# Four column tiles of one projection as a single group of seven products, and a merge by accumulating transfers

## The chip, the cores and the metric

One NeuronCore of a Trainium2 chip runs the kernel. Its engines work side by side, each through a queue of its own in a fixed order: TensorE (PE, with its weight loads shown as PEld), VectorE (DVE), ScalarE (ACT), GpSimd (POOL) and SyncE (SP), which here only issues transfers. Engines wait for one another by semaphores. The metric is the device time of the whole program in microseconds.

## The reference, cut to what matters

One layer of a hybrid encoder for 512 tokens and 2048 channels. Two branches, a sparse attention (A) and a retention (B), each give 1024 channels per token; both are projected to 2048 channels, gated, added, and go through one output projection:

```python
proj = h @ w_in
...
a_out = dsa_mixer(aq, ak, av, iq, ik, iw, positions, rel_bias) * jax.nn.silu(az)
...
b_out = retention_mixer(rq, rk, rv, ret_gn_gain) * jax.nn.silu(rz)
merged = jax.nn.sigmoid(ga) * (a_out @ w_a_out) + jax.nn.sigmoid(gb) * (b_out @ w_b_out)
r = x + merged @ w_o
return r + (p_i @ w_ple) * jax.nn.sigmoid(r @ w_ple_gate)
```

The change touches `sigmoid(ga) * (a_out @ w_a_out)`, its sum with branch B's share, and the start of `merged @ w_o`.

## The kernel before, in words

Activations lie transposed in SBUF: 128 channels on the partitions, 512 tokens along a row. Each float32 matrix is split into two float16 parts, high (`wh`, `ah`) and low (`wl`), and a product is three matmuls: high by high, high by low, low by high. ACT makes a high part (line 257 for weights, 475 and 481 for merged tiles), DVE the low part (`low_part`, line 143).

A column tile is 128 output channels; branch A's projection has 16, in the order 0, 8, 1, 9, 2, 10, ... 15 (`PAIRED`). A plain tile is `gemm`: 8 chunks of 128 input channels, three matmuls of 512 columns each (lines 337 to 339). Tiles 1 and 9, and 3 and 11, are pairs (`narrow`): `gemm_pair` with `nk=4` (line 443) splits input channels, output tiles and tokens into halves and forms the 2 by 2 block product by seven products of blocks instead of eight. Its weight blocks are sums and differences, made on the way by accumulating transfers from POOL (`add_block`, line 221) and by one DVE sum (line 268). The token side (`Xa`) is made by `a_sums` when the attention heads end. The seven products go to four PSUM banks `p`, `v`, `q`, `r`; ACT copies a bank at certain points (line 372) before PE adds to it again, and DVE combines banks and copies to the outputs (lines 378, 382, 1771). Every product is run in passes of one weight part; `RUNS` gives their order: the first two products high, the same low, the next two high, those and the fifth low, fifth and sixth high, sixth and seventh low, seventh high.

After a plain tile DVE multiplies by the gate from `sga` (line 1786) and adds branch B's share from `mbs` (line 1787); both were loaded by SP into one `B` buffer, of which there are five. When tiles k and k+8 are done, `x_step(k, 0..3)` makes the seven combinations of their token halves that the output projection needs (`sums`, lines 539 to 542, then high and low parts). The output projection is again `gemm_pair`, `nk=8`; its first group is `late`: its first four passes run over chunks 0 to 6, and then over chunk 7, which comes from tiles 7 and 15.

The order on every engine is that in which the code issues. A to-do list spreads the work: PE code calls `step()` after each chunk of a plain tile (8 a tile), after each pass of a `gemm_pair` with `nk=4` (14), and four times a pass with `nk=8` (56); each call runs what `later` made due and takes one item from the list `todo`, in which `None` is an empty place. Here `split_to(n)` makes weight parts up to unit n, and `load_to` issues their loads from SP, in order, into seven `wraw` buffers.

Of the kernel before, what the change touches and what calls it, by code (L numbers as in the profile page):

```python
# [19 lines left out]
L = 512  # L20
# [51 lines left out]

def block_kernel(tc, flag, cfg, xT, pT, posb, posq, w_in, w_v, w_r0, w_r1, w_ik, w_a, w_b, w_o, w_ple, w_gate,
                 w_gt, w_pt, fgb, tab, gains, cst, dec, out, out_a, out_b):
# [6 lines left out]
    with contextlib.ExitStack() as ctx:  # L81
# [278 lines left out]

        def gemm_pair(ids, X, done, late=False, turned=False, nk=8, more=None, compact=False):

# [6 lines left out]
            def copy(n, src):  # L369
                E[n] = U(n)  # L370
                cs = LO if compact else ALL
                act.activation(E[n][:, cs], src[:, cs], AF.Copy)  # L372

            def out(f, x, y, i, c):
                if compact:
                    return done(x[:, LO], y[:, LO], i, c, f)
                t = U("e_t")
                f(t, x, y)
                done(t[:, LO], t[:, HI], i, c)
# [12 lines left out]
            def first():  # L392
                if turned:
                    E["e1"] = U("e1")
                    act.activation(E["e1"][:, LO], p[:, LO], AF.Copy)
                else:
                    copy("e1", p)

            def second():
                if turned:  # L400
                    done(q[:, LO], E["e1"][:, LO], 0, LO)
                else:
                    out(f_q, q, E["e1"], 0, LO)
# [16 lines left out]
            for at, (n, part, ks) in enumerate(runs):  # L420
# [12 lines left out]
                for k in ks:  # L433
                    ended[n] += 1
                    x = X[PRODUCTS[n]][k]
                    if turned and isinstance(x, tuple):
                        moving = [(LO, v) for v in x[:2 - part]]
                    elif compact:
                        moving = [(LO, x[:, v]) for v in (LO, HI)[:2 - part]]
                    else:  # L440
                        moving = [(c, x[:, c])]
# [9 lines left out]
        def combos(lo, hi, name, keep=None, by=1.0, checked=False):  # L451
# [18 lines left out]
            def first_part(k):  # L470
                if k % 2 == 0:
                    one_of[0] = V2(name + "a11")
                t = X["a11"][k] = one_of[0][:, L * (k % 2):L * (k % 2) + L]
                s = lo(k)[:, LO]
                act.activation(t[:, LO], s, AF.Copy, scale=-by)
                lows.append(lambda: low_part(t[:, HI], s, t[:, LO], -by, checked))
# [167 lines left out]
        PAIRED = [m + 8 * i for m in range(8) for i in range(2)]  # L644
        u_wa.update((m, block(w_a[m], (8,))) for m in PAIRED if m % 8 not in narrow and m not in u_wa)
        u_d = [block_pair(w_o[m], w_o[m + 8]) for m in range(8)]
# [1111 lines left out]
        Xm, x_step = combos(lambda k: merged[k], lambda k: merged[k + 8], "m", by=cfg.m * un_a, checked=True)  # L1758
        for m in PAIRED:
            if m in narrow:  # L1760
                gate = []
                for n in (m, m + 8):
                    t = B("sm")
                    gate.append(t[:, 0:512])
                    merged[n] = t[:, 512:1024]
                    sp.dma_start(gate[-1], sga[n])
                    sp.dma_start(merged[n], mbs[n])
                have, pw = [0, 0], [U("wa"), U("wa")]

                def done(c0, c1, i, q, m=m, have=have, pw=pw, gate=gate):  # L1770
                    dve.tensor_add(pw[i][:, q], c0, c1)
                    have[i] += 1
                    if have[i] == 2:
                        o = merged[m + 8 * i]
                        dve.tensor_mul(pw[i], pw[i], gate[i])
                        dve.tensor_add(o, o, pw[i])

                gemm_pair(u_wn[m], Xa, done, turned=True, nk=4, more=lambda at: None)
            elif m - 8 not in narrow:
                t = B("sm")  # L1780
                s, o = t[:, 0:512], t[:, 512:1024]
                sp.dma_start(s, sga[m])
                sp.dma_start(o, mbs[m])
                merged[m] = o
                pw = gemm(u_wa[m], aparts, "ps_w")
                dve.tensor_mul(s, pw, s)
                dve.tensor_add(o, o, s)
            if m >= 8:
                k = m - 8
                gap = X_AFTER if k + 1 in narrow else X_BEHIND if k in narrow else (0, 0)  # L1790
                todo.extend([None] * gap[0])
                for i in (0, 1, 2, 3) if fast else (1, 0, 2, 3):
                    todo.extend([lambda k=k, i=i: x_step(k, i)] + [None] * gap[1])

# [409 lines left out]
OUTS_AT = (7, 7, 9, 9)  # L2204
X_AFTER, X_BEHIND = (5, 1), (2, 1)
LOOK = 3
# [20 lines left out]
def _layout(x, p, positions, w_in, norm_gain, w_a_out, w_b_out, w_o, ret_gn_gain,  # L2227
# [12 lines left out]
    o = {}  # L2240
# [14 lines left out]
    o["w_a"] = np.ascontiguousarray(tiles(np.asarray(w_a_out)[0])[:, :, A_ORDER])  # L2255
    o["w_b"] = tiles(np.asarray(w_b_out)[0])
    o["w_o"] = tiles(np.asarray(w_o)[0])
    o["w_ple"] = np.ascontiguousarray(
# [66 lines left out]
```

## Time and profile before

| | |
|---|---|
| median of 3 runs | 1543.59 us (1543.3 to 1544.23) |
| the profiled execution: time, span | 1543.44 us, 1541.6 us |
| granted TensorE clock, mean | 0.998 |
| PE busy | 1529.4 us, 99% |
| DVE busy | 1317.6 us, 85% |
| ACT busy | 970.0 us, 63% |
| POOL busy | 225.0 us, 15% |

The span runs from the first to the last instruction of the program; the time of the execution is 1.84 us longer. Matmuls are pipelined and their ends are modelled, so the pace of PE is read from starts. A row of the timeline merges like instructions that follow one another; in brackets stands the idle time of the engine ahead of it and what ended that.

### The profile page before, as it was taken

What the parts mean: (1) busy time and instruction counts of PE and PEld (TensorE: products, weight loads), DVE (VectorE), ACT (ScalarE), POOL (GpSimd) and SP (SyncE); (2) the same over time, 40 slices, a digit from 0 to 9 for tenths busy, and PEclk for the clock granted to TensorE, in tenths of its full rate; (3) what the DMA queues carried; (4) which work ended last, traced back from release to release, by engine and by line L of the source; (5) the groups of instructions that cost most, each with busy time, mean ns of one, the idle gap of its engine ahead of it and who ended that gap; (6) DMA issues with size and microseconds to landing.
All of it is one profiled execution on the core that took longest, in us unless ns stands there. A gap on an engine that the chain in (4) does not pass through costs nothing.

```text
span 1541.6 us, 27918 instructions
## 1 busy us (share of the span) xinstructions
PE 1529.4 (99%) x10433; PEld 986.7 (64%) x10433; DVE 1317.6 (85%) x2712; ACT 970.0 (63%) x1491; POOL 225.0 (15%) x261
## 2 busy tenths in 40 slices
PE   9999999999999999999999999999999999999997
PEld 5654446778878878876555666655555566547765
DVE  8899889888888888987788888788889999998975
ACT  7565545665666665687877766667633555576654
POOL 3000111111111111113431121200000111101101
PEclk9999999999999999999999999999999999999999
DMA  8436989899899899899999898999556899878974
GB/s 325 134 117 196 263 213 253 227 228 236 219 227 237 216 228 235 217 228 268 272 248 243 229 249 239 276 352 343 198 198 191 209 232 241 221 232 238 259 213 147
DMA packets 136274, 358.26 MB, mean 232 GB/s; under 512 B 22208, under 2 KB 34752, under 8 KB 136128
## 3 DMA queue, kind: packets, MB, share of 16 engines
q1 hardware_dynamic: 94368, 230.08, 43.1%
q0 software_dynamic: 28656, 101.20, 35.4%
q10 hardware_dynamic: 13104, 25.09, 4.4%
q8 instruction: 83, 1.36, 0.3%
q14 instruction: 63, 0.52, 0.1%
HBM read 311.76 MB, written 42.99 MB: 230 GB/s over the span
## 4 chain that ended last, share of the span: by engine, by line
PE 88%; DVE 6%; ACT 2%; issue 1%; DMA 1%; SPq 0%; DVEq 0%; ACTq 0%
PE ps_p L443 27%; PE ps_v L443 18%; PE ps_q L443 9%; PE ps_r L443 9%; PE ps_vn L1151 2%; PE ps_vn L1150 2%; PE ps_vn L1152 2%; PE ps_iq L339 1%; PE ps_iq L337 1%; PE ps_iq L338 1%; DVE wl L143 1%; ACT bm L1610 1%; PE ps_pg L2018 1%; PE ps_pg L2019 1%; PE ps_pg L2020 1%
## 5 line engine op out<-in xcount | busy, mean ns | idle before, releaser
L143 DVE SCALAR_TENSOR_TENSOR wl<-wraw,wh 128x1024 f16<-128x1024 f32 (+3 forms) x461 | 559.1, 1221 | 124.4 <-ACT wh L257 113.5
L257 ACT ACTIVATE wh<-wraw 128x1024 f16<-128x1024 f32 (+3 forms) x484 | 490.1, 1024 | 136.1 <-DVE wraw L268 74.8
L443 PEld LDWEIGHTS <-wh 128*128 128x128 f16 x4120 | 402.2, 98 | 239.0 <-issue 1.5
L443 PEld LDWEIGHTS <-wl 128*128 128x128 f16 x2968 | 289.4, 98 | 55.0 <-issue 0.2
L221 POOL DMA_DIRECT2D wraw<-w_in x120 | 106.4, 969 | 562.3 <-DVE wl L143 479.8
L443 PE MATMUL ps_p<-hs,wh 128*128 128x256 f16 (+1 forms) x896 | 153.2, 318 | 0.0
L372 ACT ACTIVATE e<-ps_p 128x512 f32<-128x512 f32 (+1 forms) x158 | 83.3, 527 | 91.7 <-PE ps_p L443 85.1
L443 PE MATMUL ps_p<-hs,wl 128*128 128x256 f16 x640 | 84.2, 273 | 0.0
L443 PE MATMUL ps_q<-ha,wh 128*128 128x256 f16 (+1 forms) x448 | 76.0, 318 | 0.0
L443 PE MATMUL ps_r<-hs,wh 128*128 128x256 f16 (+1 forms) x448 | 75.9, 318 | 0.0
L443 PE MATMUL ps_v<-ha,wh 128*128 128x256 f16 (+1 forms) x448 | 75.9, 318 | 0.0
L443 PE MATMUL ps_p<-ha,wh 128*128 128x256 f16 (+1 forms) x448 | 75.9, 318 | 0.0
L443 PE MATMUL ps_v<-hs,wh 128*128 128x256 f16 (+1 forms) x448 | 75.9, 318 | 0.0
L1045 ACT ACTIVATE mk<-relf,thr 128x512 f16<-128x512 f32 (+3 forms) x128 | 67.5, 553 | 1.4 <-ACT go L1501 1.2
L268 DVE TENSOR_TENSOR wraw<-wraw 128x1024 f32<-128x1024 f32 x53 | 64.9, 1225 | 1.8
L339 PEld LDWEIGHTS <-wl 128*128 128x128 f16 x396 | 38.8, 98 | 40.8 <-DVE wl L143 0.9
L337 PEld LDWEIGHTS <-wh 128*128 128x128 f16 x396 | 38.9, 98 | 36.6
L338 PEld LDWEIGHTS <-wh 128*128 128x128 f16 x396 | 38.8, 98 | 36.6
L1501 ACT ACTIVATE go<-go 128x512 f32<-128x512 f32 x40 | 25.1, 629 | 51.3 <-DVE go L1492 51.3
L221 POOL DMA_DIRECT2D wraw<-w_o x24 | 21.0, 929 | 235.5 <-DVE wl L143 101.3
L338 PE MATMUL ps_w<-bh,wh 128*128 128x512 f16 x128 | 48.5, 379 | 0.0
L339 PE MATMUL ps_w<-bh,wl 128*128 128x512 f16 x128 | 48.5, 379 | 0.0
(471 smaller groups left out, 2858.0 us busy)
## 6 DMA issues: line engine op xcount, KB each, us to landing
wraw<-w_in SPq DMA_DIRECT2D x170, 512.0 KB, 5.5
wraw<-w_in POOLq DMA_DIRECT2D x120, 512.0 KB, 7.9
wraw<-w_o SPq DMA_DIRECT2D x32, 512.0 KB, 5.4
wraw<-w_o POOLq DMA_DIRECT2D x24, 512.0 KB, 7.6
wraw<-w_gate SPq DMA_DIRECT2D x24, 512.0 KB, 5.3
wraw<-w_v SPq DMA_DIRECT2D x16, 512.0 KB, 7.4
wraw<-w_b SPq DMA_DIRECT2D x16, 512.0 KB, 6.3
wraw<-w_gate POOLq DMA_DIRECT2D x15, 512.0 KB, 7.5
```

The source lines that it names most:

```text
L143: dve.scalar_tensor_tensor(l, src, 1.0 if gain is None else gain, h, op0=OP.mult, op1=OP.subtract, **({"accum_out": column()} if checked a ...
L221: pool.dma_start(out=view(raw_tiles[r], nk, cols), in_=src[:, k0:k0 + nk, :], accum_op=OP.add)
L257: act.activation(h, raw, AF.Copy, scale=cfg.w)
L268: dve.tensor_add(raw, raw, view(raw_tiles[plus], nk, cols))
L337: pe.matmul(o, h[:, k, w], a, start=(s == order[0]), stop=False)
L338: pe.matmul(o, h[:, k, w], b, start=False, stop=False)
L339: pe.matmul(o, l[:, k, w], a, start=False, stop=(s == order[-1]))
L372: act.activation(E[n][:, cs], src[:, cs], AF.Copy)
L443: pe.matmul(o[:, co], w[:, k], src, start=(n < 4 and begin and k == 0 and j == 0), stop=(ended[n] == 2 * nk), skip_group_check=True)
L1045: act.activation(bias_e[b][i // per][:, ln * (i % per):ln * (i % per + 1)], relf[:, :ln], AF.Sign, bias=thr[:, q:q + 1])
L1150: pe.matmul(o, a[:, tok(t)], h[:, k], start=(s == 0), stop=False)
L1151: pe.matmul(o, a[:, tok(t)], l[:, k], start=False, stop=False)
```

## The change: what it does

- Tiles 4, 5, 12 and 13 are one group: `gemm_pair` with `double=True` and `nk=8`. Its output blocks are two column tiles wide; of the eight chunks of a product, four belong to the first tile and write a bank's low half, four to the second and write its high half. The weights come from a new input `w_ad`, the same numbers in another layout, in seven units made by `block_pair`.
- The pairs 1 and 3 are `compact`: high and low token parts go to the same 256 columns, and DVE combines 256 columns where it combined 512.
- Tiles 0, 8, 1, 9, 3, 11, 4, 12, 5, 13 are merged otherwise: the gated tile lies in a buffer, and POOL adds branch B's share from DRAM by an accumulating transfer (`merge`). The loads of `mbs` by SP and DVE's additions for these ten go.
- The order of the tiles is 0, 8; the group; pair 1; 2, 10; pair 3; 6, 14; 7, 15. Each set of `x_step` items has a lead of empty places and places in between (`A_TILES`).

```diff
@@ -358,7 +358,7 @@
         SPLIT_AT = {0: 3, 2: 4, 3: 4, 4: 5, 7: 6, 8: 7, 10: 8, 12: 9}
         LOAD_AT = (0, 2, 4, 6, 8, 10, 12)
 
-        def gemm_pair(ids, X, done, late=False, turned=False, nk=8, more=None, compact=False):
+        def gemm_pair(ids, X, done, late=False, turned=False, nk=8, more=None, compact=False, double=False):
 
 
 
@@ -368,12 +368,13 @@
 
             def copy(n, src):
                 E[n] = U(n)
-                cs = LO if compact else ALL
+                cs = LO if compact and not double else ALL
                 act.activation(E[n][:, cs], src[:, cs], AF.Copy)
 
             def out(f, x, y, i, c):
                 if compact:
-                    return done(x[:, LO], y[:, LO], i, c, f)
+                    cs = ALL if double else LO
+                    return done(x[:, cs], y[:, cs], i, c, f)
                 t = U("e_t")
                 f(t, x, y)
                 done(t[:, LO], t[:, HI], i, c)
@@ -390,14 +391,14 @@
                 out(f_r, r, E["e3"], 1, LO)
 
             def first():
-                if turned:
+                if turned and not compact:
                     E["e1"] = U("e1")
                     act.activation(E["e1"][:, LO], p[:, LO], AF.Copy)
                 else:
                     copy("e1", p)
 
             def second():
-                if turned:
+                if turned and not compact:
                     done(q[:, LO], E["e1"][:, LO], 0, LO)
                 else:
                     out(f_q, q, E["e1"], 0, LO)
@@ -432,11 +433,12 @@
                 begin = ended[n] == 0
                 for k in ks:
                     ended[n] += 1
-                    x = X[PRODUCTS[n]][k]
+                    x = X[PRODUCTS[n]][k % 4 if double else k]
+                    to = (LO, HI)[k // 4] if double else LO
                     if turned and isinstance(x, tuple):
-                        moving = [(LO, v) for v in x[:2 - part]]
+                        moving = [(to, v) for v in x[:2 - part]]
                     elif compact:
-                        moving = [(LO, x[:, v]) for v in (LO, HI)[:2 - part]]
+                        moving = [(to, x[:, v]) for v in (LO, HI)[:2 - part]]
                     else:
                         moving = [(c, x[:, c])]
                     for j, (co, src) in enumerate(moving):
@@ -642,7 +644,9 @@
                 u_wa[8 * (n - 14)] = block(w_a[8 * (n - 14)], (8,))
         assert not to_make
         PAIRED = [m + 8 * i for m in range(8) for i in range(2)]
-        u_wa.update((m, block(w_a[m], (8,))) for m in PAIRED if m % 8 not in narrow and m not in u_wa)
+        four = [2 * FOUR + t for t in range(2)] if fast else []
+        u_ad = block_pair(w_ad[0], w_ad[1]) if fast else None
+        u_wa.update((m, block(w_a[m], (8,))) for m in PAIRED if m % 8 not in (*narrow, *four) and m not in u_wa)
         u_d = [block_pair(w_o[m], w_o[m + 8]) for m in range(8)]
         u_p = [block(w_ple[:, 8 * q:8 * q + 8], (8,)) for q in range(MF // 4)]
         u_e = [block(w_gate[m], K8) for m in range(cfg.me)]
@@ -1756,41 +1760,89 @@
 
         merged = {}
         Xm, x_step = combos(lambda k: merged[k], lambda k: merged[k + 8], "m", by=cfg.m * un_a, checked=True)
-        for m in PAIRED:
-            if m in narrow:
-                gate = []
-                for n in (m, m + 8):
-                    t = B("sm")
-                    gate.append(t[:, 0:512])
-                    merged[n] = t[:, 512:1024]
-                    sp.dma_start(gate[-1], sga[n])
-                    sp.dma_start(merged[n], mbs[n])
-                have, pw = [0, 0], [U("wa"), U("wa")]
-
-                def done(c0, c1, i, q, m=m, have=have, pw=pw, gate=gate):
-                    dve.tensor_add(pw[i][:, q], c0, c1)
-                    have[i] += 1
-                    if have[i] == 2:
-                        o = merged[m + 8 * i]
-                        dve.tensor_mul(pw[i], pw[i], gate[i])
-                        dve.tensor_add(o, o, pw[i])
-
-                gemm_pair(u_wn[m], Xa, done, turned=True, nk=4, more=lambda at: None)
-            elif m - 8 not in narrow:
+
+        def x_steps_of(k, lead=0, between=0):
+            todo.extend([None] * lead)
+            for i in (0, 1, 2, 3) if fast else (1, 0, 2, 3):
+                todo.extend([lambda i=i: x_step(k, i)] + [None] * between)
+
+        def merge(m, o):
+            merged[m] = o
+            pool.dma_start(out=o, in_=mbs[m], accum_op=OP.add)
+
+        def gate_tile(m):
+            t = U("sg")
+            sp.dma_start(t, sga[m])
+            return t
+
+        def one_tile(m):
+            away = fast and m % 8 in AWAY
+            if away:
+                s = gate_tile(m)
+            else:
                 t = B("sm")
                 s, o = t[:, 0:512], t[:, 512:1024]
                 sp.dma_start(s, sga[m])
                 sp.dma_start(o, mbs[m])
                 merged[m] = o
-                pw = gemm(u_wa[m], aparts, "ps_w")
-                dve.tensor_mul(s, pw, s)
+            pw = gemm(u_wa[m], aparts, "ps_w")
+            dve.tensor_mul(s, pw, s)
+            if away:
+                merge(m, s)
+            else:
                 dve.tensor_add(o, o, s)
-            if m >= 8:
-                k = m - 8
-                gap = X_AFTER if k + 1 in narrow else X_BEHIND if k in narrow else (0, 0)
-                todo.extend([None] * gap[0])
-                for i in (0, 1, 2, 3) if fast else (1, 0, 2, 3):
-                    todo.extend([lambda k=k, i=i: x_step(k, i)] + [None] * gap[1])
+
+        def half_pair(m):
+            gate = [gate_tile(n) for n in (m, m + 8)]
+            have, pw = [0, 0], [U("wa"), U("wa")]
+
+            def done(x, y, i, c, f):
+                f(pw[i][:, c], x, y)
+                have[i] += 1
+                if have[i] == 2:
+                    dve.tensor_mul(pw[i], pw[i], gate[i])
+                    merge(m + 8 * i, pw[i])
+
+            gemm_pair(u_wn[m], Xa, done, turned=True, nk=4, more=lambda at: None, compact=True)
+
+        def four_tiles():
+            tiles = [[m + 8 * i for m in four] for i in range(2)]
+            g = {}
+
+            def load(i):
+                for m in tiles[i]:
+                    g[m] = gate_tile(m)
+
+            later(12, lambda: load(0))
+            later(24, lambda: load(1))
+            o = [B("wd")[:, 0:1024].rearrange("p (t c) -> p t c", t=2) for _ in range(2)]
+            have = [0, 0]
+
+            def mul(i, t):
+                m = tiles[i][t]
+                dve.tensor_mul(o[i][:, t], o[i][:, t], g[m])
+                merge(m, o[i][:, t])
+
+            def done(x, y, i, c, f):
+                x, y = (v.rearrange("p (t c) -> p t c", t=2) for v in (x, y))
+                f(o[i][:, :, c], x, y)
+                have[i] += 1
+                if have[i] == 2:
+                    for t in range(2):
+                        later(2 + 2 * t, lambda t=t: mul(i, t))
+
+            gemm_pair(u_ad, Xa, done, turned=True, compact=True, double=True)
+
+        for kind, k, ks in A_TILES if fast else [("one", k, ((k, 0, 0),)) for k in range(8)]:
+            if kind == "one":
+                one_tile(k)
+                one_tile(k + 8)
+            elif kind == "half":
+                half_pair(k)
+            else:
+                four_tiles()
+            for v in ks:
+                x_steps_of(*v)
 
 
         rt = {}
@@ -2202,7 +2254,10 @@
 QUERIES = 18
 TURN = 22
 OUTS_AT = (7, 7, 9, 9)
-X_AFTER, X_BEHIND = (5, 1), (2, 1)
+FOUR = 2
+AWAY = (0, 4, 5, 1, 3)
+A_TILES = (("one", 0, ((0, 10, 4),)), ("four", 4, ((4, 10, 3), (5, 2, 1))), ("half", 1, ((1, 1, 1),)),
+           ("one", 2, ((2, 0, 2),)), ("half", 3, ((3, 5, 1),)), ("one", 6, ((6, 0, 0),)), ("one", 7, ((7, 0, 0),)))
 LOOK = 3
 A_SUMS, A_SUMS_LAST = ((6, 0), (8, 2), (10, 3)), ((2, 0), (3, 2), (4, 3))
 A_ORDER = (0, 2, 4, 6, 1, 3, 5, 7)
@@ -2254,6 +2309,8 @@
                        axis=1).reshape(KT, 128, 512).transpose(1, 0, 2))
     o["w_a"] = np.ascontiguousarray(tiles(np.asarray(w_a_out)[0])[:, :, A_ORDER])
     o["w_b"] = tiles(np.asarray(w_b_out)[0])
+    o["w_ad"] = np.ascontiguousarray(o["w_a"].reshape(2, 4, 2, 128, 2, 4, 128)[:, FOUR].transpose(0, 2, 3, 1, 4, 5)
+                                     .reshape(2, 128, 16, 128))
     o["w_o"] = tiles(np.asarray(w_o)[0])
     o["w_ple"] = np.ascontiguousarray(
         np.asarray(w_ple)[0].reshape(2, 128, 16, 128).transpose(1, 2, 0, 3).reshape(128, 32, 128))
```

## Rows read from the trace of the kernel before

**Rows 1.** The page: span, and each engine's busy time.
```profile
span 1541.6 us, 27918 instructions
...
PE 1529.4 (99%) x10433; PEld 986.7 (64%) x10433; DVE 1317.6 (85%) x2712; ACT 970.0 (63%) x1491; POOL 225.0 (15%) x261
```

**Rows 2.** Busy time of stretches of the span: the whole stage, and five microseconds.
```profile
core 0: us, PE busy (x) PEld busy (x) DVE busy (x) ACT busy (x) POOL busy (x), PEclk, DMA share, GB/s
1125.00:1207.00 82.00, 81.56 (x433) 42.12 (x432) 71.46 (x164) 30.26 (x50) 1.73 (x2) 1.00 0.62 199
1140.00:1145.00 5.00, 5.00 (x39) 3.62 (x37) 3.14 (x10) 2.18 (x5) 0.00 (x0) 1.00 0.14 52
```

**Rows 3.** Timeline of PE: start, duration, instructions; pairs 1 and 3, output projection.
```profile
1136.36 1.03 PE L443 MATMUL ps_v<-as,wh 128*128 128x512 f16 x4
...
1138.97 1.04 PE L443 MATMUL ps_q<-ah,wh 128*128 128x256 f16 x8
1139.84 1.03 PE L443 MATMUL ps_r<-as,wh 128*128 128x512 f16 x4
...
1164.28 1.46 PE L443 MATMUL ps_p<-as,wh 128*128 128x256 f16 x8 [0.44 <-ACT e L372]
1165.58 0.38 PE L337 MATMUL ps_w<-ah,wh 128*128 128x512 f16 x1
...
1207.02 1.67 PE L443 MATMUL ps_v<-ms,wh 128*128 128x512 f16 x7
...
1211.96 0.38 PE L443 MATMUL ps_v<-ms,wh 128*128 128x512 f16 x1 [0.22 <-DVE ms L143]
```

**Rows 4.** Timeline of DVE: after tile 8, and tiles 14, 7, 15.
```profile
1136.56 0.69 DVE L1786 TENSOR_TENSOR sm<-ps_w,sm 128x512 f32<-128x512 f32 x1 [1.39 <-PE ps_w L339]
1137.29 0.69 DVE L1787 TENSOR_TENSOR sm<-sm 128x512 f32<-128x512 f32 x1
1137.90 0.42 DVE L539 TENSOR_TENSOR t<-sm 128x256 f32<-128x256 f32 x1
...
1197.90 0.69 DVE L1786 TENSOR_TENSOR sm<-ps_w,sm 128x512 f32<-128x512 f32 x1
...
1200.38 0.42 DVE L539 TENSOR_TENSOR t<-sm 128x256 f32<-128x256 f32 x1
...
1202.75 0.69 DVE L143 SCALAR_TENSOR_TENSOR ms<-t,ms 128x512 f16<-128x512 f32 x1 [0.70 <-ACT ms L481]
1203.37 0.08 DVE L143 DVE_READ_ACCUMULATOR ms<-t,ms 128x1 f32 x1
1203.37 0.42 DVE L143 SCALAR_TENSOR_TENSOR ma<-sm,ma 128x256 f16<-128x256 f32 x1
...
1204.94 0.69 DVE L1786 TENSOR_TENSOR sm<-ps_w,sm 128x512 f32<-128x512 f32 x1
...
1207.41 0.69 DVE L1786 TENSOR_TENSOR sm<-ps_w,sm 128x512 f32<-128x512 f32 x1
...
1208.74 1.22 DVE L143 SCALAR_TENSOR_TENSOR wl<-wraw,wh 128x1024 f16<-128x1024 f32 x1
...
1209.88 0.42 DVE L539 TENSOR_TENSOR t<-sm 128x256 f32<-128x256 f32 x1
```

**Rows 5.** Groups of the page: busy, mean ns of one; idle before, releaser.
```profile
L268 DVE TENSOR_TENSOR wraw<-wraw 128x1024 f32<-128x1024 f32 x53 | 64.9, 1225 | 1.8
...
L378 DVE TENSOR_TENSOR e_t<-ps_v,e 128x512 f32<-128x512 f32 x39 | 26.7, 685 | 0.4 <-PE ps_v L443 0.4
```

**Rows 6.** Timeline of ACT: conversions of merged tile 6, then weights; a bank copy.
```profile
1202.09 0.63 ACT L481 ACTIVATE ms<-t 128x512 f16<-128x512 f32 x1 [4.34 <-DVE t L542]
1202.62 0.40 ACT L475 ACTIVATE ma<-sm 128x256 f16<-128x256 f32 x1
1202.93 0.61 ACT L481 ACTIVATE ma<-sm 128x512 f16<-128x512 f32 x1
...
1212.82 0.60 ACT L372 ACTIVATE pv<-ps_v 128x512 f32<-128x512 f32 x1 [0.29 <-PE ps_v L443]
1213.32 1.05 ACT L257 ACTIVATE wh<-wraw 128x1024 f16<-128x1024 f32 x1
```

**Rows 7.** POOL's accumulating transfers of 256 KB, 1005 to 1082: count, issue time, landing.
```profile
L221 POOL DMA_DIRECT2D wraw<-w_a x6: 853/864/882, 1009.7 to 1079.3; - x6
...
DMA to landing us min/median/max: 4.5/6.8/7.8
```

**Rows 8.** Transfer queues: packets, MB, share of 16 engines' span (q0 is POOL's).
```profile
q1 hardware_dynamic: 94368, 230.08, 43.1%
q0 software_dynamic: 28656, 101.20, 35.4%
```

More of the change, by code (lines that the diff above doesn't have):

```diff
@@ L70, with block_kernel @@
 RET_Y = 2.0 ** 5
-def block_kernel(tc, flag, cfg, xT, pT, posb, posq, w_in, w_v, w_r0, w_r1, w_ik, w_a, w_b, w_o, w_ple, w_gate,
+def block_kernel(tc, flag, cfg, xT, pT, posb, posq, w_in, w_v, w_r0, w_r1, w_ik, w_a, w_b, w_ad, w_o, w_ple, w_gate,
                  w_gt, w_pt, fgb, tab, gains, cst, dec, out, out_a, out_b):
@@ L470, in first_part @@
             def first_part(k):
-                if k % 2 == 0:
-                    one_of[0] = V2(name + "a11")
-                t = X["a11"][k] = one_of[0][:, L * (k % 2):L * (k % 2) + L]
+                if k // 2 not in one_of:
+                    one_of[k // 2] = V2(name + "a11")
+                t = X["a11"][k] = one_of[k // 2][:, L * (k % 2):L * (k % 2) + L]
                 s = lo(k)[:, LO]
```

## The prediction

> **What bounds the kernel now.** I read the page first: TensorE (PE) is busy 99% of the span, VectorE (DVE) 85%, GpSimd (POOL) 15% [rows 1]. Then the busy time of the stretch that the change touches, branch A's projection at 1125 to 1207 us: PE 81.56 of 82.00 us, DVE 71.46, transfers 62% of their engines [rows 2]. PE sets the pace; DVE, at 87%, has no room for a queue that stalls. Next the timeline of PE [rows 3]: the reader is to see that it waits twice only, 0.44 us in pair 3 (for ScalarE's, ACT's, copy of a bank) and 0.22 us at 1211.96, where the output projection needs the last merged tiles. So all that can be had by better overlap is 0.66 us; the rest must come from fewer columns. Last the timeline of DVE at the end of the stage [rows 4]. It runs in the written order and waits at what depends on PE: tile 14's multiplication (1197.90), a low part, one tile's sums and low parts (1200.38 to 1204.94), tile 7's (1204.94, ready at about 1202), a low part, tile 15's at 1207.41, 0.39 us after PE finished it. From there 4.55 us of fixed chain lead to PE's restart at 1211.96.
>
> **Columns.** A plain tile is 24 matmuls of 512 columns. Between 1165.58 and 1207.02 eight tiles take 41.44 us [rows 3], 5.18 each, 20.72 for the four. The group has 7 products x 8 x 3 = 168 matmuls of 256 columns; eight such take 0.87 us [rows 3], so 168 take 18.27. **PE gains 2.45 us.** Pairs 1 and 3 keep 84 x 0.109 = 9.13 us each: where one 512-column matmul held both parts, two of 256 do.
>
> **DVE's work.** Away go ten additions at 0.65 (0.61 to 0.69) and, in the two pairs, six 512-wide sums at 0.69: 6.5 + 4.1 us. Added are three more low parts and one weight sum of 1024 columns at 1.14 each, and four 512-wide combinations at 0.72: 4.6 + 2.9 us [rows 4, 5]. Net 3.1 us less. That is no gain by itself, since PE sets the pace; it buys slack. ACT gets three weight conversions (0.95 pitch [rows 6]) and four bank copies (0.5) more; it is busy 30 of 82 us [rows 2]. SP loses ten loads; the weights loaded stay 2 MB. POOL gets thirteen transfers at 0.87 us of its time in an engine that is almost idle here (1.73 us, [rows 2]). Behind them in POOL's queue stand the sums of the output projection's weights, wanted 30 us later: nothing. An accumulated byte holds the transfer engines twice as long as a plain one (35.4% for 101 MB, 43.1% for 230 MB [rows 8]): 4.2 MB more of the one at 0.35% of the span per MB, 2.6 MB less of the other at 0.19%, some 15 us of all sixteen in a stretch where they are idle 38% of 82 us [rows 2], so hidden, and at most a later landing.
>
> **The new wait.** Before, DVE followed its addition with the subtractions on the merged tile at once (1137.29, 1137.90 [rows 4]). Now these wait for an accumulating transfer to land, and everything behind them in DVE's queue waits too. The nearest rows are the six accumulating transfers of the same 256 KB: 4.5, median 6.8, at most 7.8 us from issue to landing [rows 7]. The 4.5 was issued on transfer engines that moved little; in 1140 to 1145 they are 14% busy [rows 2], but one 512 KB accumulation of the group's own weights is under way. I take 5.0, nearer to the low end.
>
> Call the group's start 0. Tile 8's product is done at 0.93 (1136.36 to 1137.29 [rows 3, 4]), so it lands at T = 5.9 (5.4 to 8.7). The subtractions of tile 0 are at step 11 of the group's 56, and in DVE's queue only one low part stands between, so DVE idles from about 2 to T. Behind them: four subtractions 1.6; then ACT, which waits for them as well, has two conversions (0.54, 0.31), two bank copies (0.50 each), one more conversion (0.52) and the fifth product's weights (0.95), 3.3 together; its low part on DVE 1.14. So the fifth low part is ready at T + 6.1. Then the weight sum 1.14, three low parts 1.57, a combination 0.72 and two low parts of weights 2.28: the seventh is ready at T + 11.8. PE wants it after six high and six low passes, 6 x 1.74 + 6 x 0.87 = 15.7. Each us of T above 3.9 stalls PE by a us: **2.0 us** (1.5 to 4.8).
>
> A rule stands beside these rows. The Trainium skill, "DMA: Bandwidth & Descriptors", section "Anatomy of one DMA", gives a transfer from GpSimd about 2 us plus its bytes at 436 GB/s, estimated 2.6 us for 256 KB. By it T would be 3.5 and there would be no stall. The trace does not agree: none of its six landed under 4.5.
>
> The tiles of the group: its last combinations leave DVE some 1.75 us behind when pair 1 starts; two combinations (1.44) and tile 12's multiplication (0.72) end at 3.9 after that start, landing 8.9, subtractions to 10.5 (9.9 to 13.2). PE needs nothing of it in pair 1 or tiles 2 and 10, but the queue carries on late: to the end of tile 1's subtractions stand 15.6 us (four combinations of 256 columns at 0.42, two multiplications at 0.72, two of these with their additions at 1.33, two low parts of weights 2.28, two sets of subtractions 3.2, eight low parts of merged tiles 4.36), so 26.1. Then ACT has 1.37 of conversions before the copy of the sixth bank (0.38): 27.9. PE wants that copy in pair 3 at 9.13 + 10.36 + 7.83 = 27.3, a stall of 0.6 in place of the 0.44 of [rows 3]: **+0.1 us** (-0.4 to +3.0).
>
> **The end of the stage.** This is the term I trust most. One item of the to-do list runs per step: 56 steps in the group, 14 in a pair, 8 in a plain tile. From the group's end the list holds 26 + 10 (tiles 4, 5) + 9 + 12 + 13 (1, 2, 3) + 4 (6) = 74 items, with 76 steps to run them. So the last items, tile 6's four, come at steps 11 to 14 of the last 16, and tile 3's at 3, 5, 7 and 9: two tiles' split work falls into the last pair of column tiles, where one fell before. Between tile 14's multiplication and tile 15's DVE has: two merges 2.66, two low parts of weights 2.28, two sets of subtractions 3.2, eight low parts of merged tiles 4.36 (per tile three of 512 columns at 0.61 and one of 256 at 0.35), and twice 0.67 to wait for ACT's conversion, as at 1202.09 to 1202.75 [rows 4, 6]: 13.8 us. Tile 14's starts 0.2 after PE ends it, PE gives 10.36 for the last pair; so tile 15's starts 3.7 after PE instead of 0.39. The 4.55 us behind it are the same, and PE's own work before it needs tile 7 is the same 4.72 (1207.02 to 1211.74). **+3.3 us** at PE's restart. Both ACT waits filled by other work: 2.0; DVE entering 1 us late, as at 1197.90: 4.3.
>
> **Sum.** -2.45 + 2.0 + 0.1 + 3.3 = +3.0 us. The profiled execution took 1543.44 us (span 1541.6, the rest lies around it), 0.15 under the median. So **1546.4 us**, 0.2% above; 0.2% (3.1 us) is about what a measurement of this kernel tells from no change. The likeliest case's own range is 1544 to 1551.
>
> **Rivals.**
> - *The transfers land in time* (T below 3.9, so landing within 3.0 us). For it: engines nearly idle at 1140 to 1145; against it: 4.5 is the least of six. Then -2.45 - 0.44 + 3.3 = +0.4, **1543.8**. The page's rule named above would make this case. Chance 0.20.
> - *The relief wins.* DVE's 3.1 us less means tile 15's multiplication still starts within 0.4 us of PE's end, and nothing stalls: -2.45 - 0.66 = -3.1, **1540.3**. It decides from the point at which the work between tiles 14 and 15 fits into 10.5 us. For it: DVE's load over the stage does fall. Against it: my count of steps puts 13.8 us there. Chance 0.15, two thirds of it beyond 0.2%.
> - *The lag spreads.* Landing as at the slow rows (7.8 us), so stalls 4.8 and 3.0 and a late entry to the end (4.3): +9.7, **1553**. For it: these rows; against it: they were taken with engines full. Chance 0.10.
> - *My forecast*, some of the gain eaten by waits: 0.55, about half of it above 0.2%.
>
> Faster 0.10, within 0.2% 0.52, slower 0.38. The range that leaves out no more than 2 in 10 runs from 1541.0, among the relief's, to 1551.0, short of the spreading lag's.
>
> **What would show it.** Right: 168 matmuls of the group in about 18.3 us plus waits; DVE idle in the group for an accumulating transfer; tile 15's multiplication some 3.7 us after PE's last plain matmul; PE idle 3.5 us, not 0.22, ahead of the first product's last chunk. Wrong: landings of 3 us; tile 3's split work already done when tile 14's multiplication comes; PE's restart 5 us after the last plain tile as before.

## The result and the profile after

The changed kernel takes 1561.28 us (median of 5 runs, 1560.36 to 1562.19) where before takes 1543.59 (1543.27 to 1544.81): a ratio of 1.0113, 95% interval 1.0098 to 1.0128. It is slower by 17.7 us; the forecast was 1546.4, and 1551 the upper end of the range. The profiled spans, 1558.6 and 1541.6 us, differ by 17.0.

The page of the changed kernel: PE works 1.9 us longer than in [rows 1], though it has fewer columns to do, and its share falls to 98%.

```profile
span 1558.6 us, 28143 instructions
...
PE 1531.3 (98%) x10537; PEld 998.0 (64%) x10537; DVE 1314.3 (84%) x2707; ACT 973.4 (62%) x1498; POOL 235.9 (15%) x274
```

Busy time in stretches of the changed kernel, and under it one stretch of the kernel before:

```profile
core 0: us, PE busy (x) PEld busy (x) DVE busy (x) ACT busy (x) POOL busy (x), PEclk, DMA share, GB/s
1125.00:1207.00 82.00, 70.02 (x481) 47.49 (x480) 53.68 (x122) 27.99 (x47) 11.37 (x13) 0.94 0.68 181
1140.00:1145.00 5.00, 5.00 (x49) 4.48 (x47) 0.39 (x2) 0.00 (x0) 0.00 (x0) 1.00 0.76 166
...
1160.00:1175.00 15.00, 15.00 (x110) 10.49 (x108) 3.84 (x7) 1.15 (x3) 4.41 (x5) 1.00 1.04 319
...
1185.00:1190.00 5.00, 0.00 (x0) 0.00 (x0) 4.93 (x12) 0.47 (x1) 0.00 (x0) 0.63 0.56 153
1190.00:1195.00 5.00, 2.90 (x14) 2.02 (x14) 4.82 (x15) 2.09 (x7) 0.00 (x0) 0.50 0.44 126
```

```profile
1160.00:1175.00 15.00, 14.56 (x82) 7.90 (x81) 13.57 (x33) 5.44 (x11) 0.86 (x1) 1.00 0.63 185
```

Three things to see. In the stage DVE is busy 53.68 us where it was busy 71.46 [rows 2]: it did not lose that much work, it stood still and did the work later. In 1160 to 1175 DVE works 3.84 us of 15, and the transfer engines are full (1.04; before, 0.63). And after PE's idle 1185 to 1190 the granted clock is 0.50, the 1.2 GHz level.

The timeline of PE, which answers to [rows 3]: the group, pair 1's start, pair 3, tile 6's start, the output projection.

```profile
1136.14 1.91 PE L445 MATMUL ps_v<-as,wh 128*128 128x256 f16 x16
...
1147.23 1.05 PE L445 MATMUL ps_r<-as,wl 128*128 128x256 f16 x8 [1.31 <-DVE wl L143]
1150.75 1.05 PE L445 MATMUL ps_p<-as,wl 128*128 128x256 f16 x8 [2.47 <-DVE wl L143]
...
1159.09 1.04 PE L445 MATMUL ps_v<-as,wh 128*128 128x256 f16 x8
...
1178.62 1.04 PE L445 MATMUL ps_v<-as,wh 128*128 128x256 f16 x8
...
1192.10 2.72 PE L445 MATMUL ps_p<-as,wh 128*128 128x256 f16 x12 [8.07 <-ACT e L372]
1194.61 2.42 PE L445 MATMUL ps_v<-ah,wh 128*128 128x256 f16 x12
1196.86 1.47 PE L445 MATMUL ps_p<-as,wh 128*128 128x256 f16 x12
1198.17 0.38 PE L337 MATMUL ps_w<-ah,wh 128*128 128x512 f16 x1
...
1218.89 1.46 PE L445 MATMUL ps_v<-ms,wh 128*128 128x512 f16 x6
1221.64 0.38 PE L445 MATMUL ps_v<-ms,wh 128*128 128x512 f16 x1 [1.29 <-DVE ms L143]
...
1227.61 0.59 PE L445 MATMUL ps_v<-ms,wh 128*128 128x512 f16 x1 [2.56 <-DVE ms L143]
...
1228.85 2.79 PE L445 MATMUL ps_q<-ma,wh 128*128 128x512 f16 x8
1231.47 1.89 PE L445 MATMUL ps_r<-ms,wh 128*128 128x512 f16 x8
```

In the kernel before, the output projection comes to its fourth bank here:

```profile
1214.46 1.89 PE L443 MATMUL ps_r<-ms,wh 128*128 128x512 f16 x8
```

From start to start the 17 us can be laid out. The group lasts 22.95 us: 18.27 of columns as forecast, 4.7 lost, so +2.2 against four plain tiles. Pair 1 and tiles 2 and 10 take 19.53, as they would have. Pair 3 takes 19.55 where 9.13 are work and 0.44 was waited before: +10. PE waits 8.07 us. Behind that the slow clock makes two passes of twelve matmuls some 2.1 us longer (2.51 and 2.25 from start to start where such a pass takes 1.31), but this cost next to nothing: the pair's last pass wants one more copy from ACT, which ended at 1196.68 (the row at 1196.32 below), and at full clock PE would have been ready for it at 1194.72 and waited. So the 10 us are the lateness of that copy. Tiles 6 to 15 take 20.72, as before. From the start of the output projection to its fourth bank the time is 12.58; before, the same passes took 7.44 (1207.02 in [rows 3] to 1214.46): +5.1, with 1.29 + 2.56 - 0.22 = 3.6 of waits and the rest slow clock (0.72 granted in 1226 to 1232). Sum 17.3; the group starts 0.2 us earlier.

The timeline of DVE (line 1789 multiplies a plain tile, 1823 a tile of the group, 541 and 542 begin the steps on the merged tiles):

```profile
1144.68 0.42 DVE L542 TENSOR_TENSOR t<-sg 128x256 f32<-128x256 f32 x1 [4.61 <-DMA sg<-mbs]
...
1159.22 1.29 DVE L1823 TENSOR_TENSOR wd<-wd,sg 128x512 f32<-128x512 f32 x2
...
1161.73 1.29 DVE L1823 TENSOR_TENSOR wd<-wd,sg 128x512 f32<-128x512 f32 x2
...
1173.60 0.43 DVE L541 TENSOR_TENSOR t<-wd 128x256 f32<-128x256 f32 x1 [9.01 <-DMA wd<-mbs]
1178.01 0.42 DVE L542 TENSOR_TENSOR t<-wd 128x256 f32<-128x256 f32 x1 [3.98 <-DMA wd<-mbs]
...
1223.07 0.68 DVE L1789 TENSOR_TENSOR sm<-ps_w,sm 128x512 f32<-128x512 f32 x1
```

The timeline of POOL, which issues the accumulating transfers (line 1771) and the weight sums (line 221), and then the landing of all ten:

```profile
1137.44 0.86 POOL L1771 DMA_DIRECT2D sg<-mbs  x1 [1.94 <-DVE sg L1789]
1163.10 0.88 POOL L221 DMA_DIRECT2D wraw<-w_o  x1 [24.79 <-DVE wd L1823]
1163.71 2.06 POOL L1771 DMA_DIRECT2D wd<-mbs  x2
1171.85 0.87 POOL L1771 DMA_DIRECT2D wd<-mbs  x1 [6.08 <-issue]
...
DMA to landing us min/median/max: 4.0/6.4/11.3
```

Tile 4 is multiplied by about 1159.9. Its transfer is issued 3.8 us later, since the first weight sum of the output projection stands ahead of it in POOL's queue, and lands at 1173.6, 9.9 us after its issue. (The sum's row names DVE as what released it; by the times it was the sum's own plain load, issued at 1156.43 and landed at 1162.43.) Tile 12 is multiplied by about 1162.4. POOL then issues nothing for 6.08 us with no cause in the trace, sends this transfer at 1171.85, and it lands at 1178.0: 15.6 us after its product, where the forecast took 5.0.

How full the transfer engines were from issue to landing of three of the ten, those of tiles 8, 4 and 3 (columns as above):

```profile
1137.44:1144.66 7.22, 7.22 (x69) 6.47 (x67) 1.49 (x3) 1.06 (x1) 0.86 (x1) 1.00 0.92 212
...
1163.71:1173.58 9.87, 9.87 (x69) 6.53 (x67) 0.42 (x1) 0.38 (x1) 2.93 (x4) 1.00 1.07 309
1198.69:1202.68 3.99, 3.99 (x20) 1.77 (x19) 3.96 (x11) 1.01 (x2) 1.76 (x2) 1.00 0.45 66
```

At a share of 0.45 the landing took 4.0 us, at 0.92 and 1.07 it took 7.2 and 9.9. The share alone does not fix it (tile 12's 6.1 us fell at 1.07 too), and no run changed the other loads beside these transfers: that the load makes the landing long is read from these rows, not tested.

The timeline of ACT shows how that reaches PE: the copies of the banks, wanted by PE, stand behind conversions of merged tiles, which wait for DVE.

```profile
1189.53 0.63 ACT L483 ACTIVATE ms<-t 128x512 f16<-128x512 f32 x1 [6.01 <-DVE t L544]
...
1191.41 0.36 ACT L372 ACTIVATE pv<-ps_v 128x256 f32<-128x256 f32 x1
1191.67 0.37 ACT L372 ACTIVATE e<-ps_p 128x256 f32<-128x256 f32 x1
...
1196.32 0.36 ACT L372 ACTIVATE e<-ps_p 128x256 f32<-128x256 f32 x1
```

### The profile page after: what moved, and what is told of

Its sections match the earlier page's. It is cut to its first block, busy times and chain, and to the rows that moved or that the text cites. A ratio compares the mean times of both kernels' runs of the same rounds, so it can differ in the third digit from the quotient of the medians.

```text
span 1558.6 us, 28143 instructions
## 1 busy us (share of the span) xinstructions
PE 1531.3 (98%) x10537; PEld 998.0 (64%) x10537; DVE 1314.3 (84%) x2707; ACT 973.4 (62%) x1498; POOL 235.9 (15%) x274
## 4 chain that ended last, share of the span: by engine, by line
PE 88%; DVE 6%; ACT 3%; issue 2%; DMA 1%; POOL 0%; DVEq 0%; ACTq 0%; POOLq 0%
PE ps_p L445 27%; PE ps_v L445 18%; PE ps_q L445 9%; PE ps_r L445 9%; PE ps_vn L1156 2%; PE ps_vn L1155 2%; PE ps_vn L1154 2%; PE ps_iq L337 1%; PE ps_iq L338 1%; PE ps_iq L339 1%; DVE wl L143 1%; ACT bm L1614 1%; PE ps_pg L2070 1%; PE ps_pg L2072 1%; PE ps_pg L2071 1%
## 5 line engine op out<-in xcount | busy, mean ns | idle before, releaser
L445 PEld LDWEIGHTS <-wh 128*128 128x128 f16 x4264 | 417.7, 98 | 250.9 <-issue 14.0
L337 PEld LDWEIGHTS <-wh 128*128 128x128 f16 x364 | 35.7, 98 | 32.7
L338 PEld LDWEIGHTS <-wh 128*128 128x128 f16 x364 | 35.6, 98 | 32.6
L338 PE MATMUL ps_w<-bh,wh 128*128 128x512 f16 x128 | 48.5, 379 | 0.0
L337 PE MATMUL ps_w<-bh,wh 128*128 128x512 f16 x128 | 48.5, 379 | 0.0
```

Of the source, the lines that this page charges most:

```text
L337: pe.matmul(o, h[:, k, w], a, start=(s == order[0]), stop=False)
L338: pe.matmul(o, h[:, k, w], b, start=False, stop=False)
L445: pe.matmul(o[:, co], w[:, k], src, start=(n < 4 and begin and k == 0 and j == 0), stop=(ended[n] == 2 * nk), skip_group_check=True)
```

## The experiments

The theory from these rows: the accumulating transfers land late, DVE stands still for them in its queue, and that is most of the loss; the end of the stage is a second, smaller term. Rivals: POOL's queue order, POOL's halts, the list of steps. All times are medians; before took 1543.5 to 1543.6 us beside them.

**e1: branch B's share loaded by SP and added by DVE.**

```diff
-            pool.dma_start(out=o, in_=mbs[m], accum_op=OP.add)
+            dve.tensor_add(o, o, share[m])
...
+            share[m] = U("mb")
+            sp.dma_start(share[m], mbs[m])
```

> All merges by a load on SP and an addition on VectorE again; the group, the compact pairs, the order of tiles and the places of the steps stay as after the change. Theory (VectorE stands waiting for accumulating transfers, and TensorE then waits for VectorE): the stalls in the group (4.7 us) and in pair 3 (10.4 us with the slower clock) go, the crowded end of about 4 us stays; 1543 to 1547 us. Rival (the group itself, its weights or the crowding of steps costs the time): 1555 us or more.

Measured: 1546.20 us, ratio 1.0019 (1.0009 to 1.0028). With this list of steps the accumulating transfers cost 15.1 of the 17.7 us. All of PE's waits that are left, on its timeline:

```profile
1183.93 1.47 PE L445 MATMUL ps_p<-as,wh 128*128 128x256 f16 x12 [0.87 <-ACT e L372]
...
1209.86 0.38 PE L445 MATMUL ps_v<-ms,wh 128*128 128x512 f16 x1 [2.44 <-DVE ms L143]
...
1215.84 0.38 PE L445 MATMUL ps_v<-ms,wh 128*128 128x512 f16 x1 [2.56 <-DVE ms L143]
```

The group has none and runs at the forecast's columns; the clock stays at 1.00. -2.45 + 0.4 + 4.8 = 2.8 is what the medians show (2.7).

**e2: the steps later, the transfers kept.**

```diff
-A_TILES = (("one", 0, ((0, 10, 4),)), ("four", 4, ((4, 10, 3), (5, 2, 1))), ("half", 1, ((1, 1, 1),)),
-           ("one", 2, ((2, 0, 2),)), ("half", 3, ((3, 5, 1),)), ("one", 6, ((6, 0, 0),)), ("one", 7, ((7, 0, 0),)))
+A_TILES = (("one", 0, ((0, 24, 2),)), ("four", 4, ((4, 28, 1), (5, 0, 1))), ("half", 1, ((1, 0, 1),)),
+           ("one", 2, ((2, 0, 1),)), ("half", 3, ((3, 0, 1),)), ("one", 6, ((6, 0, 1),)), ("one", 7, ((7, 0, 0),)))
```

> As after the change, with the same transfers, but the split steps of tile 0 stand at steps 25 to 34 of the group and those of tiles 4 and 5 only from step 29 after the group on, one empty place between all that follow. Theory: no item of VectorE's queue waits for a transfer for long, so the group and pair 3 lose under 1 us each, the end loses 4 to 5 us as more steps lie there; 1544 to 1551 us. Rival (the accumulating transfers cost by their load on the engines, wherever VectorE stands): 1556 us or more.

Measured: 1550.7 us, ratio 1.0043 (1.0026 to 1.0060). The waits shrink to 0.33 us in the group and 1.52 in pair 3, so both came from steps that ask too early: 10.6 of the 17.7 us come back with every transfer kept, though the ten land no sooner than in the change (4.2, median 7.2, at most 12.4 us). Work that starts later ends later: at the end PE waits 5.55 and 0.94 us, and the granted clock falls behind that.

**e3: the weight sum behind the group's four transfers in POOL's queue.**

```diff
-                    later(12 if i in in_big else 0, lambda i=i, plus=plus: add_block(i, plus))
+                    later(12 if i in in_big else 20 if i in held else 0, lambda i=i, plus=plus: add_block(i, plus))
...
+        held.add(units[u_d[0][0]][0])
```

> As after the change, but the first sum of the output projection's weights is issued 20 steps later, behind the four merges of the group in POOL's queue. Theory A (the merges stand behind that sum): tile 12's share lands 6 to 8 us earlier, pair 3 loses 2 us instead of 10, the group's 4.7 us stay; 1550 to 1554 us. Theory B (POOL halts after two transfers in flight, whatever they are): it halts ahead of the third merge again and less than 3 us are won; 1558 us or more.

Measured: 1556.35 us, ratio 1.0080 (1.0063 to 1.0097): 4.9 us come back, less than theory A had and more than theory B. Pair 3 alone lasts 13.34 us for 19.55 (1181.02 to 1194.36), 6.2 less, with two waits left, of 2.00 and 1.86 us. But the group lasts 25.08 us for 22.95: behind waits of 1.16 and 2.48 us the granted clock is 0.50 in 1150 to 1155, and sixteen matmuls take 3.62 us for 1.91. The groups of e4, e6, e7 and e8, where PE waits at the same two places, are slowed in the same way, to 25.0 to 25.7 us. By the profiled executions, then, comparing whole times with the changed kernel shows these edits as worth 2 to 3 us less than they save elsewhere.

```profile
1152.54 3.62 PE L445 MATMUL ps_p<-as,wh 128*128 128x256 f16 x16
...
1161.49 1.04 PE L445 MATMUL ps_v<-as,wh 128*128 128x256 f16 x8
```

On DVE's timeline the two shares are there at 1170.25 and 1174.33. That is some 3.5 us earlier by the clock, and 5.8 and 6.1 us earlier counted from the start of pair 1 (1161.49 here, 1159.09 in the change):

```profile
1170.25 0.42 DVE L541 TENSOR_TENSOR t<-wd 128x256 f32<-128x256 f32 x1 [3.26 <-DMA wd<-mbs]
1174.33 0.42 DVE L542 TENSOR_TENSOR t<-wd 128x256 f32<-128x256 f32 x1 [3.66 <-DMA wd<-mbs]
```

Tile 4's transfer, issued at 1162.14, still takes 8.1 us, and POOL still halts, 4.72 us ahead of the fourth.

**e4: twice the space for POOL's descriptors.** One activation buffer of 28 goes to make room for it.

```diff
-    nc = bacc.Bacc("TRN2", target_bir_lowering=False, num_devices=1, dynamic_dma_scratch_size=1024)
+    nc = bacc.Bacc("TRN2", target_bir_lowering=False, num_devices=1, dynamic_dma_scratch_size=2048)
```

> As after the change, with twice the scratch for POOL's transfer descriptors (2048 instead of 1024 bytes) and one activation buffer less (27 for 28) to make room. Theory B (the 6.1 us in which POOL waits for nothing shown, ahead of the third merge, is a full descriptor ring): the third merge is issued right behind the second, tile 12's share lands some 5 us earlier; 1552 to 1556 us. Theory A (only the order in the queue and the transfer engines count): within 2 us of the change, 1559 to 1563 us.

Measured: 1560.36 us, ratio 1.0108 (1.0091 to 1.0125): as the changed kernel. POOL issues all four without a halt (first row), and by the clock DVE gets the shares no sooner (the other two):

```profile
1165.12 3.87 POOL L1771 DMA_DIRECT2D wd<-mbs  x4
...
1175.26 0.42 DVE L541 TENSOR_TENSOR t<-wd 128x256 f32<-128x256 f32 x1 [7.30 <-DMA wd<-mbs]
1179.26 0.42 DVE L542 TENSOR_TENSOR t<-wd 128x256 f32<-128x256 f32 x1 [3.58 <-DMA wd<-mbs]
```

Here too the slow clock hides something: the group lasts 25.71 us. Counted from pair 1's start (1162.47) the shares are 1.7 and 2.1 us sooner than in the change, and pair 3 lasts 17.62 us, 1.9 less. So the halt belongs to the descriptor space, and it is a small part of what makes the share late.

**e5: e1 with only tile 6's steps in the last pair of column tiles.**

```diff
...
+A_TILES = (("one", 0, ((0, 10, 4),)), ("four", 4, ((4, 6, 1), (5, 0, 1))), ("half", 1, ((1, 0, 1),)),
+           ("one", 2, ((2, 3, 1),)), ("half", 3, ((3, 4, 1),)), ("one", 6, ((6, 0, 0),)), ("one", 7, ((7, 0, 0),)))
```

> Like e1 (branch B's share loaded by SP and added by DVE, no accumulating transfers), and the leads of the steps changed so that only tile 6's four steps fall into the last pair of column tiles. Theory (after e1 what is left is the column gain and the two waits at the end of the stage): e1's waits of 2.44 and 2.56 us ahead of the output projection's passes shrink to about 0.2 to 0.7 in sum, so the span is some 4.5 us under e1's 1545.2, about 1541, and 1 to 3 us under that of before. Rival: the waits at the end come from another thing than the place of the steps (ACT's conversions or the weights' low parts); then they stay near 5 us and the time near e1's 1546.2.

Measured: 1549.53 us, ratio 1.0037 (1.0023 to 1.0051). The waits at the end are gone as expected, so the end is a matter of the list; but 1.52 and 5.06 us of waiting for ACT's copies stand in pairs 1 and 3, where the steps now crowd, and the granted clock is 0.50 in 1185 to 1190. The span I expected, 1541, came out as 1547.7.

**e6: only the group's four shares on DVE.**

```diff
+            if m % 8 in four:
+                return dve.tensor_add(o, o, share[m])
             pool.dma_start(out=o, in_=mbs[m], accum_op=OP.add)
...
+            if m % 8 in four:
+                share[m] = U("mb")
+                sp.dma_start(share[m], mbs[m])
```

> Only the shares of the group's four tiles (4, 5, 12, 13) are loaded by SP and added by DVE; the other six keep the accumulating transfers. Theory (the merges of the group behind the weight sum in POOL's queue set the long wait): PE's 8.1 us in pair 3 falls to 1 to 2, with it goes the slow clock behind it, the stalls of 1.3 and 2.5 us inside the group (tile 8's share) stay, and the time is near 1551. Rival (the transfer engines are simply overloaded, whichever tiles use them): the wait moves to tiles 1 and 9 and the time stays above 1556.

Measured: 1553.08 us, ratio 1.0063 (1.0047 to 1.0078). Pair 3's wait falls from 8.07 to 0.87 us, the group's stay (2.21 and 2.48, and it lasts 25.50 us), the end keeps 1.02 and 2.56, and the granted clock falls behind both. The long wait is that of the group's own four transfers.

**e7: e3 and e4 together.**

> The two edits of e3 and e4 together: the first weight sum of the output projection behind the group's four merges in POOL's queue, and twice the descriptor space, so that POOL issues all four merges without a halt. Theory (what remains is the transfers' own time beside busy transfer engines): tile 12's and 13's shares still land 7 to 9 us after their issue, and the time stays within 3 us of e3's 1556.4. Rival (halt and order together made the lateness): landings of about 5 us as taken in the prediction, no wait over 1 us in pair 3, and a time near 1550.

Measured: 1556.13 us, ratio 1.0078 (1.0063 to 1.0093), as e3. All four are issued by 1167; tile 4's takes 8.1 us (1162.60 to 1170.69) and tile 12's is there at 1175.29. With queue order and halt both out of the way the landing is still 8 us and more; in 1160 to 1175 the transfer engines are full (1.02) here too. Four runs can now be laid side by side. Counted from pair 1's start, DVE uses tile 12's share after 18.92 us in the change, 16.79 in e4, 13.52 in e7 and 12.84 in e3; pair 3 lasts 19.55, 17.62, 14.02 and 13.34. It follows that share us for us, 0.5 to 0.8 behind.

**e8: the list of the changed kernel, with tile 6's steps alone at the end and the transfers kept.**

```diff
-A_TILES = (("one", 0, ((0, 10, 4),)), ("four", 4, ((4, 10, 3), (5, 2, 1))), ("half", 1, ((1, 1, 1),)),
-           ("one", 2, ((2, 0, 2),)), ("half", 3, ((3, 5, 1),)), ("one", 6, ((6, 0, 0),)), ("one", 7, ((7, 0, 0),)))
+A_TILES = (("one", 0, ((0, 10, 4),)), ("four", 4, ((4, 10, 3), (5, 2, 1))), ("half", 1, ((1, 0, 0),)),
+           ("one", 2, ((2, 0, 0),)), ("half", 3, ((3, 4, 1),)), ("one", 6, ((6, 0, 0),)), ("one", 7, ((7, 0, 0),)))
```

> The changed kernel with all its accumulating transfers; only the empty places between the steps of tiles 1, 2 and 3 are taken out or moved, so that tile 6's four steps alone fall into the last pair of column tiles. Theory (the end term is a matter of the to-do list alone): the waits of 1.3 and 2.6 us at the start of the output projection, and the slow clock behind them, go almost wholly; the stalls in the group and in pair 3 stay; time about 1556. Rival (DVE comes late to the end because of the transfers): the waits at the end stay above 3 us, and the time above 1559.

Measured: 1569.79 us, ratio 1.0173 (1.0157 to 1.0188): 8.5 us slower than the change, against both expectations. PE waits 3.86 us among tiles 6 to 15 (first row, for a weight's high part) and 3.46 at the end, each with the granted clock at 0.50 behind it. DVE's timeline tells why (the other two):

```profile
1218.68 0.61 PE L337 MATMUL ps_w<-ah,wh 128*128 128x512 f16 x1 [3.86 <-ACT wh L257]
...
1208.02 0.42 DVE L541 TENSOR_TENSOR t<-wa 128x256 f32<-128x256 f32 x1 [1.42 <-DMA wa<-mbs]
1214.85 0.43 DVE L542 TENSOR_TENSOR t<-wa 128x256 f32<-128x256 f32 x1 [6.40 <-DMA wa<-mbs]
```

Tile 11's transfer is issued at 1205.86 and lands 9 us later, and now the steps on it come at once. In the changed kernel the same transfer landed after 4.0 us, at 1205.54, and was first used at 1211.81: the late steps that cost 5 us at the end left it 6 us of room. Why it took 9 us here stays open.

**e9 and e10: a third list, first with all shares on DVE, then with the transfers of tiles 1 and 9 alone.**

```diff
...
+A_TILES = (("one", 0, ((0, 10, 4),)), ("four", 4, ((4, 6, 2), (5, 0, 2))), ("half", 1, ((1, 0, 1),)),
+           ("one", 2, ((2, 0, 2),)), ("half", 3, ((3, 0, 1),)), ("one", 6, ((6, 0, 0),)), ("one", 7, ((7, 0, 0),)))
```

> As e1 and e5 (no accumulating transfers), with a third list of steps, which spreads them more evenly than e5's: two empty places between the steps of tiles 4, 5 and 2, none ahead of those of 1, 2 and 3. e1's waits were 0.9 us in pair 3 and 5.0 at the end, e5's 6.6 in pairs 1 and 3 and none at the end. Theory (without the transfers VectorE, busy some 94% in this stretch, is itself the bound, so the list only moves the wait): PE's waits from the group to the output projection again sum to 4 to 7 us and the time is 1545 to 1549. Rival (each wait is a fault of its list): the sum is under 2.5 us and the time 1541 to 1543, under that of before.

> e9's list, with the accumulating transfers kept for tiles 1 and 9 alone, whose steps come some 12 us after pair 1 ends; the other eight shares are added by VectorE. Theory (a transfer costs nothing where its tile is wanted later than it lands, 6 to 10 us, and relieves VectorE of 0.7 us each): VectorE shows no wait for a transfer, PE's waits are 1 to 2 us less than e9's, the time as much under e9's. Rival (any of these transfers makes VectorE or POOL late): a wait of VectorE for these two tiles of 3 us or more, and a time above e9's.

Measured: e9 1546.33 us, ratio 1.0018 (1.0009 to 1.0027); e10 1545.60 us, ratio 1.0013 (1.0004 to 1.0022). PE's waits in e9:

```profile
1164.24 1.47 PE L445 MATMUL ps_p<-as,wh 128*128 128x256 f16 x12 [1.51 <-ACT e L372]
1182.95 1.47 PE L445 MATMUL ps_p<-as,wh 128*128 128x256 f16 x12 [1.64 <-ACT e L372]
1187.36 1.47 PE L445 MATMUL ps_p<-as,wh 128*128 128x256 f16 x12 [1.63 <-ACT e L372]
...
1215.12 0.38 PE L445 MATMUL ps_v<-ms,wh 128*128 128x512 f16 x1 [1.01 <-DVE ms L143]
```

Their sum is 5.8 us; under three lists it was 5.9 (e1), 6.6 (e5) and 5.8. Under these three the wait moved and its sum hardly changed. In e10 DVE waits for no transfer, and PE's waits sum to 4.9, 0.9 less than e9's where 1 to 2 were expected: where a tile is wanted well after its landing, the transfer costs nothing that these rows show. That it gains is not shown: 0.7 us lie between the medians, and the runs of the two overlap. e10 is the fastest with the group in it, 15.7 us under the change, and not under before.

## Why the prediction was wrong, point by point

- **Columns, -2.45: right.** The passes last 1.74 and 0.87 us as taken, and in e1 the group runs without a wait.
- **The wait in the group, +2.0: the mechanism right, T mis-sized.** "Each us of T above 3.9 stalls PE by a us" holds: tile 8's share is used at 1144.68, so T = 8.5, which gives 4.6; 4.7 was measured, though PE begins to wait sooner than forecast, at the fourth product's low part (1147.23). T = 5.9 was taken since the transfer engines were "14% busy" in 1140 to 1145. That row is of before; after the change the same five microseconds show 76%. The rows of before held the price: from issue to landing, five of the six in [rows 7] had transfer engines at a share of 0.99 to 1.05 beside them and took 6.3 to 7.8 us, and the one of 4.5 had 0.69. The upper bound, 8.7, held.
- **Pair 3, +0.1 (-0.4 to +3.0): this is the step that failed**, with +10. The "landing 8.9" counts from pair 1's start; tile 12's share was used 18.9 after it. The chain behind it was right: the copy that PE's last pass waits for, forecast for 27.9, ended 37.6 after that start, and these 10 us are what PE lost, most of them as a wait for the copy ahead of it, which the prediction did not look at (in e3, e4 and e7 pair 3 shrinks as the share comes sooner). One sentence of the prediction hides it: "Behind them in POOL's queue stand the sums of the output projection's weights [...] nothing." I asked who stands behind the merges and not behind whom they stand. e3 puts the price of that order at 6.2 us of pair 3's 10 (4.9 of the whole time, since its group was slowed). The rest is landing, priced at 5.0 as for one transfer: with the order out of the way tile 12's share, the third of four, took 9.4 us (e3) and 10.1 (e7) beside full transfer engines. The prediction's own estimate of 15 us of transfer time "in a stretch where they are idle 38%" was an average over 82 us; in the 15 us that mattered they were at 1.04.
- **The end, +3.3 (2.0 to 4.3): right in kind, near in size.** Tile 15's multiplication starts at 1223.07, about 4.2 us after PE's last plain tile (forecast 3.7), and the waits grow by 3.6; slow clock makes it 5.1. e5 shows that it is the list's doing.
- **The chances.** "The transfers land in time" was not near: the ten took 4.0 to 11.3 us. The Trainium skill, "DMA: Bandwidth & Descriptors", section "Anatomy of one DMA", fits a transfer from GpSimd by about 2.0 us plus its bytes at 436 GB/s, an estimated 2.6 us for 256 KB. This trace does not agree, its least is 4.0. "The lag spreads" named what happened but bounded the landing by 7.8 us, the slowest of six that were spread over 70 us [rows 7].
- **What the group costs without transfers.** In e1, e5 and e9 waits of some 6 us remain under each of three lists. That VectorE is the bound is argued, not shown: it is busy 54.95 of 60.5 us in e9 (1154.5 to 1215), and several times it waits 0.2 to 0.7 us for ACT's conversion. A list or an order of tiles that frees PE altogether was not found, nor excluded. The most it could give is small: 2.45 of columns and the 0.66 that PE waited in [rows 3], 3.1 us or 0.2%.

## What to carry to other kernels

An addition moved from a busy engine to a transfer is a latency put into that engine's queue: price its landing from the stretch as it will be after the change, with all that is issued beside it, and look at what stands ahead of it on the issuing queue as well as behind. A to-do list that makes one wait vanish may be what hides another: move the steps and the transfers they depend on together. Before reshaping a stage that PE already fills to 99%, write down the most that can be had; here it was 3.1 us against stalls of 17.

## What the runs showed of the hardware that was not expected

- Behind PE's idle 8 us the granted clock is 0.50 in 1190 to 1195 and 0.85 in 1195 to 1200. What this costs depends on what PE waits for next: two passes took 2.1 us longer there and lost almost nothing, since a copy came later still; in e3's group, with waits of 3.64 us in sum for 3.78, the slow clock cost 2.1 us. Short waits did not always do this: 1.31 and 2.47 us in the changed kernel left the clock at 1.00 (1145 to 1160), 1.16 and 2.48 in e3 brought it to 0.50 (1150 to 1155). What tells them apart stays open.
- POOL stops after a few accumulating transfers in a row, for 6.1 us here, 7.1 in e2 and 4.7 in e3, and does not with twice the descriptor space (e4, e7). By that pair 3 gained 1.9 us in e4 and nothing in e7 against e3, and the whole time nothing clear of noise.
